# Squares behind both heads' products, probabilities' low parts last, and the merged half turned one tick sooner, in a two-layer hybrid encoder

## The chip, the cores and the metric

The kernel runs on one core of a Trainium2 chip. Its time is the device time of one execution in microseconds (us). The engines are named as in the profile: PE multiplies matrices, PEld is its weight load, DVE is the vector engine, ACT the scalar engine, POOL is GpSimd, and SP issues most transfers.

## The reference

256 tokens of 1024 channels pass through two layers. The part that matters here, for each layer:

```python
u = rms_norm(h, g_mix_pre)
(gq, gk, gv, gg, ra_f, ra_b, aq, ak, av, gate_a, gate_b) = jnp.split(u @ w_in, offsets, axis=-1)
# branch A: gated linear attention (GLA), 4 heads of 256 values, both directions summed
o_gla = rms_norm(o_f + o_b, g_gla_out).reshape(b, s, GLA_VAL)   # a root for each head and token
branch_a = (o_gla * jax.nn.silu(gg)) @ w_o_gla
# branch B: 8 query heads of 128 on 2 key/value heads
pr = jax.nn.softmax(sc, axis=-1)
out = jnp.einsum('bkgqs,bskd->bqkgd', pr, v)
branch_b = out @ w_o_attn
# merge
mixed = jax.nn.sigmoid(gate_a) * branch_a + jax.nn.sigmoid(gate_b) * branch_b
h = h + rms_norm(mixed @ w_out, g_mix_post)
```

A SwiGLU feed-forward part and a per-layer embedding follow; the change does not touch them.

## The kernel before

Tokens lie in two halves (`hf`) of 128. Every matrix product of full accuracy is three products: each operand is split into a high part (rounded to the matrix engine's 32-bit format) and the low rest, and high × high, high × low and low × high are added up in one PSUM tile. `split` (L133) makes the parts: ACT casts the high one, DVE subtracts to get the low one. `mm3` (L105) multiplies one pair of operands so; `passes` (L121) does it for a list of pairs, and puts the products of one operand's low parts behind all the others. A weight arrives by DMA as 128x1024 pieces, is split into wh and wl, and is used in blocks of twelve matmuls of 128x512 (four pieces of the contraction by three products).

The work of a layer stands in the program in the order rq, kv, gqk, v, gg, gate, merge, wout, ffnin, ffnout, ple; the names in the profile end in these (acc_0wout is a PSUM accumulator of layer 0's output projection). Beside this main row run tasks, Python generators that are taken a step further by `tick()`: it is called twice in each block of twelve matmuls, once in the middle and once at the end, and a task that has yielded n goes on n ticks later. So attention (`at`), the GLA outputs (`gla`) and the out-gate are threaded between the projections' blocks. A scheduler of the framework then orders the instructions on each engine, so that a step that the program moves by a line may end elsewhere in an engine's row. Eight PSUM banks serve all accumulators; the framework keeps two engines from using one tile at the same time by waits.

The three places that the change touches:

- **GLA outputs.** `outputs(hf, pr)` takes one PSUM tile (aux_0gla) for the two heads of a pair: six matmuls of 128x256 for each head, each followed by an ACT Square with a sum over the row (L1345). Both sums go to POOL for the root (`inv_sqrt`, L465 and L466), and DVE multiplies each head by its root and a gain (`scale_gain`, L515) into big_0gla. There are four such tiles in a layer. Behind them the out-gate (`out_gate`) waits for all outputs and the attention: ACT loads its table and takes the Sigmoid of gg (L1406), DVE multiplies (L126) gg and big_0gla into it, and PE transposes the result (L447, aux_0gg) for the product with w_o_gla.
- **Attention.** `attend` multiplies the values with the transposed probabilities, whose halves (mid_0at) were split just before: two `mm3` for the two halves of the keys, into aux_0at; four such tiles in a layer.
- **Merge.** `merge(1)` multiplies the second branch by its gate and adds (L1469) into the first; a task `turn` then waits `WAIT_MIX[hf]` ticks and transposes this quarter (L447, aux_0merge), and splits it into big_0merge, the operand of the output projection acc_0wout.

Of the kernel before, what the change touches and what calls it, by code (L numbers as in the profile page):

```python
# [13 lines left out]
AF = mybir.ActivationFunctionType  # L14
# [3 lines left out]
P = 128  # L18
# [8 lines left out]
WAIT, WAIT_FIRST, WAIT_FFN, WAIT_BLOCK = 6, 4, 4, 6  # L27

WAIT_NEXT, WAIT_IN, WAIT_H = (7, 9), ((6, 9), (6, 6)), ((3, 5), (3, 5))
WAIT_MIX = 4, 6  # L30
WAIT_SPREAD = 12
W = dict(r=5, z=6, s0=4, s=3, s1=9, o0=1, o=1, k=4, q=3, a0=1, a1=4, a2=4, a3=1, g=6)

# [26 lines left out]
def trunk_kernel(ctx: ExitStack, tc: tile.TileContext, a: dict, out: bass.AP):  # L60
# [25 lines left out]
    def big(dt=F32):  # L86
        return bigp.tile([P, 2048], dt, tag="big", name=nm("big"))

    def mid(dt=F32):
        return b4p.tile([P, 1024], dt, tag="mid", name=nm("mid"))  # L90

    def acc():
        return accp.tile([P, 512], F32, tag="acc", name=nm("acc"))

    def aux():
        return accp.tile([P, 512], F32, tag="acc", name=nm("aux"))
# [4 lines left out]
    def small(n, tag, bufs=None):  # L101
        return smp.tile([P, n], F32, tag=tag, name=nm(tag), **({"bufs": bufs} if bufs else {}))

    def mm(o, lhsT, rhs, start, stop):
        return nc.tensor.matmul(o, lhsT, rhs, start=start, stop=stop)  # L105

    def mm3(o, l, r, start, stop):
        (lh, ll), (rh, rl) = l, r
        mm(o, lh, rh, start, False)
        mm(o, lh, rl, False, False)  # L110
        mm(o, ll, rh, False, stop)

    def passes(o, parts, start, stop, fresh=False, between=None, **kw):

        ps = [((xh, yh), (xh, yl), (xl, yh)) if fresh else ((xh, yh), (xl, yh), (xh, yl)) for (xh, xl), (yh, yl) in parts]
        seq = [p for t in ps for p in t[:2]] + [t[2] for t in ps]
        for n, (x, y) in enumerate(seq):  # L120
            nc.tensor.matmul(o, x, y, start=start and n == 0, stop=stop and n == len(seq) - 1, **kw)  # L121
            if between is not None and 2 * (n + 1) == len(seq):
                between()
# [7 lines left out]
    def split(hi, lo, src):  # L131

        return nc.scalar.copy(hi, src), nc.vector.tensor_tensor(out=lo, in0=src, in1=hi.bitcast(F32), op=ALU.subtract)  # L133
# [325 lines left out]
    def inv_sqrt(t, n, mul, add, eps=None):  # L459

        with in_turn():
            if eps is None:
                nc.gpsimd.tensor_scalar(out=t, in0=t, scalar1=mul, scalar2=add, op0=ALU.mult, op1=ALU.add)
            else:
                nc.gpsimd.tensor_scalar(out=t, in0=t, scalar1=eps, scalar2=mul, op0=ALU.add, op1=ALU.mult)  # L465
        last_pow[0] = nc.gpsimd.tensor_tensor(out=t, in0=t, in1=neghalf[:, :n], op=ALU.pow)  # L466
# [47 lines left out]
    def scale_gain(out, in0, r, g):  # L514
        nc.vector.scalar_tensor_tensor(out=out, in0=in0, scalar=r, in1=g, op0=ALU.mult, op1=ALU.mult)  # L515

    def halves(t):
        return [t[:, j * 512 : (j + 1) * 512] for j in range(2)]
# [205 lines left out]
    def project_t(sp):  # L724

        o = [acc(), acc()]
        for kh in range(2):
            wmode(o, sp, kh * 4, ws.take(), kh == 0, kh == 1)
            ws.done()
        return o  # L730

    def project(sp):

        o = [acc(), acc()]
        for kh in range(2):
            w = ws.take()
            for hf in range(2):
                amode(o[hf], sp, hf, kh * 4, w, kh == 0, kh == 1)
            ws.done()
        return o  # L740
# [81 lines left out]
    ss = [small(2, "ss") for _ in range(2)]  # L822
# [179 lines left out]
    for l in range(DEPTH):  # L1002
# [104 lines left out]
        o = {}  # L1107
# [18 lines left out]
        kTh, kTl, avh, avl = (kv4[:, i * 512 : (i + 1) * 512] for i in range(4))  # L1126
# [39 lines left out]
        def softmax(g, hf, q):  # L1166
            qh, ql, sc = q
            pr_ = mid().rearrange("p (h k) -> p h k", k=T)
            for b in range(2):
                s_ps = aux()  # L1170
                for i in range(2):
                    hs = slice((2 * b + i) * P, (2 * b + i + 1) * P)
                    gs = slice(g * T, (g + 1) * T)
                    mm3(s_ps[:, i * T : (i + 1) * T], (qh[:, hs], ql[:, hs]), (kTh[:, gs], kTl[:, gs]), True, True)
                mx = small(2, "mx")
                nc.vector.tensor_reduce(
                    out=mx, in_=s_ps.rearrange("p (h k) -> p h k", k=T), axis=AX.X, op=ALU.max
                )
                nc.vector.scalar_tensor_tensor(
                    out=mx, in0=mx, scalar=-1.0, in1=sc[:, 2 * b : 2 * b + 2], op0=ALU.mult, op1=ALU.mult  # L1180
                )
                sm = small(2, "sm")
                for i in range(2):
                    hd = 2 * b + i
                    last_exp[0] = nc.scalar.activation(
                        pr_[:, hd, :], s_ps[:, i * T : (i + 1) * T], AF.Exp,
                        bias=mx[:, i : i + 1], scale=sc[:, hd : hd + 1], accum_out=sm[:, i : i + 1],
                    )
                nc.vector.reciprocal(sm, sm)
                for i in range(2):  # L1190
                    hd = 2 * b + i
                    nc.vector.tensor_scalar(
                        out=pr_[:, hd, :], in0=pr_[:, hd, :], scalar1=sm[:, i : i + 1], scalar2=None, op0=ALU.mult
                    )
            return pr_

        def turn_p(pr_):
            res = []
            for s in range(2):
                ps = aux()  # L1200
                for i in range(4):
                    nc.tensor.transpose(ps[:, i * P : (i + 1) * P], pr_[:, i, s * P : (s + 1) * P], ident)
                pT = halves(mid(F32R))
                split(pT[0], pT[1], ps)
                res.append(pT)
            return res

        def attend(g):
            qs = []
            for hf in range(2):  # L1210
                yield W["q"]
                ps = aux()
                for i in range(4):
                    hd = 4 * g + i
                    nc.tensor.transpose(ps[:, i * P : (i + 1) * P], qrs[hf][:, hd * P : (hd + 1) * P], ident)
                qh, ql = halves(mid(F32R))
                split(qh, ql, ps)
                qs.append((qh, ql, qss[hf][:, 4 * g : 4 * g + 4]))
            keys.need()
            yield W["a0"]  # L1220
            prs = []
            for hf in range(2):
                prs.append(softmax(g, hf, qs[hf]))
                yield W["a1"]
            for hf in range(2):
                pT = turn_p(prs[hf])
                yield W["a2"]
                o = aux()
                for s in range(2):
                    vs = slice(s * 256 + g * P, s * 256 + (g + 1) * P)  # L1230
                    mm3(o, (avh[:, vs], avl[:, vs]), pT[s], s == 0, s == 1)
                aT.put(o, 4 * g, 4, hf * P, P)
                yield W["a3"]

        def attention():
            for g_ in range(2):
                part[0] = f"{l}at{g_}"
                yield from attend(g_)
# [9 lines left out]
        for x in range(2):  # L1248
            o = project_t(uT)
# [81 lines left out]
        on = big().rearrange("p (s c) -> p s c", s=2)  # L1331

        def outputs(hf, pr):

            o = aux()
            ss = small(8, "hss")
            for i in range(2):
                hd = 2 * pr + i
                c = slice(hd * 256, (hd + 1) * 256)
                oh = o[:, i * 256 : (i + 1) * 256]  # L1340
                for s in range(2):

                    idx = hf if s == hf else (2 if s == 0 else 3)
                    mm3(oh, [t[:, hd, idx, :] for t in sc], [t[:, s, c] for t in v], s == 0, s == 1)
                nc.scalar.activation(  # L1345
                    on[:, hf, c], oh, AF.Square, scale=1.0 / 16.0, accum_out=ss[:, i : i + 1]
                )
            inv_sqrt(ss[:, 0:2], 2, 1.0, EPS, eps_out[hf])
            for i in range(2):
                hd = 2 * pr + i  # L1350
                scale_gain(
                    on[:, hf, hd * 256 : (hd + 1) * 256], o[:, i * 256 : (i + 1) * 256], ss[:, i : i + 1], ggla
                )
# [39 lines left out]
        for j in range(2):  # L1393
            o = project(uT)
# [69 lines left out]
        def merge(br):  # L1464
            def then(j, hf, o):
                sl = [s[:, hf, j * 512 : (j + 1) * 512] for s in sgate[: br + 1]]
                vmul(sl[br], o, sl[br])
                if br == 1:
                    nc.vector.tensor_tensor(out=sl[0], in0=sl[0], in1=sl[1], op=ALU.add)  # L1469

                    def turn():
                        yield WAIT_MIX[hf]
                        transpose_in(mixT, sl[0], 4 * j, 4, hf)
# [57 lines left out]
        for hf in range(2):  # L1531
            ws.lend = hf == 1
            for b in range(2):
                o = acc()
# [51 lines left out]
        o = []  # L1586
# [140 lines left out]
```

## Time and profile before

| | us |
|---|---|
| three runs | 922.91, 920.76, 922.87 |
| their median | 922.87 |
| the profiled execution: own time | 921.4 |
| its span | 919.3 |
| PE busy in the span | 910.1 |
| DVE busy | 786.2 |
| ACT busy | 584.7 |
| POOL busy | 105.1 |

The span goes from the first to the last instruction of the profiled execution; 2.1 us of that execution's own time lie around it. The granted clock of the matrix engine was 0.997 of full speed. In the rows of the timeline the columns are start, duration, engine, line, operation, written tile and read tiles, shapes and the number of instructions in the group; the bracket at the end is the engine's idle time ahead of the group, with what ended it. Matmuls overlap in their pipeline, so a group of n takes n − 1 distances between starts and one duration.

### The profile page before, as it was taken

Reading aid. Unit: us, or ns where it says so; the run is one execution under the profiler, and the core shown is the slowest. Engines: PE = TensorE matmul, PEld = TensorE weight load, DVE = VectorE, ACT = ScalarE, POOL = GpSimd, SP = SyncE. Lnnn points to the kernel's source line nnn. Section 1 sums busy time; section 2 is a strip of 40 time slices with the busy share of each in tenths; the row PEclk is TensorE's granted clock in tenths of the full one; section 3 lists DMA queues with packets and bytes.
Section 4 is the critical chain, followed back from the end, with each engine's and each line's share of the span. In section 5 each row is a group of like instructions: output and inputs, shape, how many; then the busy total and the mean of one; then the engine's idle time right before and its main releaser. Section 6 shows DMA issues by size and latency. Waiting matters only on the chain.

```text
span 919.3 us, 12437 instructions
## 1 busy us (share of the span) xinstructions
PE 910.1 (99%) x4674; PEld 775.9 (84%) x4674; DVE 786.2 (86%) x1007; ACT 584.7 (64%) x970; POOL 105.1 (11%) x156
## 2 busy tenths in 40 slices
PE   9999999999999999999999999999999999999996
PEld 8998888888888888888899988888888788888886
DVE  6898979987669998999779789799876899989885
ACT  6688767564467565566676687675644766565563
POOL 3610212310000000000334002210001000000000
PEclk9999999999999999999999999999999999999998
DMA  8564445657385655657567424455573846556361
GB/s 280 192 209 136 138 138 189 212 184 250 104 293 183 215 194 185 246 167 254 175 255 230 138 92 140 135 183 183 186 255 121 279 165 215 213 174 223 135 232 46
DMA packets 88679, 173.44 MB, mean 189 GB/s; under 512 B 3422, under 2 KB 26470, under 8 KB 88108
## 3 DMA queue, kind: packets, MB, share of 16 engines
q1 hardware_dynamic: 88316, 172.27, 55.5%
q8 instruction: 36, 0.59, 0.3%
q10 hardware_dynamic: 304, 0.40, 0.1%
q14 instruction: 23, 0.19, 0.1%
HBM read 169.50 MB, written 3.15 MB: 188 GB/s over the span
## 4 chain that ended last, share of the span: by engine, by line
PE 93%; DVE 2%; ACT 1%; issue 1%; DMA 1%; POOL 1%; POOLq 0%; ACTq 0%; DVEq 0%; SPq 0%
PE acc_0ffnin L121 12%; PE acc_1ffnin L121 11%; PE acc_1gate L121 7%; PE acc_0gate L121 7%; PE acc_0ffnin L105 7%; PE acc_1ffnin L105 7%; PE acc_1rq L121 3%; PE acc_0gqk L121 2%; PE acc_0wout L121 2%; PE acc_1gqk L121 2%; PE acc_0ple L121 2%; PE acc_0v L121 2%; PE acc_1merge L121 2%; PE acc_0merge L121 2%; PE acc_1ple L121 2%; PE acc_0gg L121 2%
## 5 line engine op out<-in xcount | busy, mean ns | idle before, releaser
L105 PE MATMUL acc_0ffnin<-wh_0ffnin,big_0ffnin 128*128 128x512 f32 x176 | 57.0, 393 | 0.0
L105 PE MATMUL acc_1ffnin<-wh_1ffnin,big_1ffnin 128*128 128x512 f32 x176 | 56.9, 392 | 0.0
L133 ACT CAST wh_1ffnin<-raw_1ffnin 128x1024 fp32r<-128x1024 f32 x38 | 38.5, 1049 | 25.7 <-PE acc_1ffnin L105 10.3
L133 ACT CAST wh_0ffnin<-raw_0ffnin 128x1024 fp32r<-128x1024 f32 x38 | 38.2, 1048 | 24.5 <-PE acc_0ffnin L105 9.2
L133 DVE TENSOR_TENSOR wl_1ffnin<-raw_1ffnin,wh_1ffnin 128x1024 fp32r<-128x1024 f32 x38 | 44.9, 1219 | 7.9 <-ACT wh_1ffnin L133 7.6
L133 DVE TENSOR_TENSOR wl_0ffnin<-raw_0ffnin,wh_0ffnin 128x1024 fp32r<-128x1024 f32 x38 | 44.7, 1220 | 8.0 <-ACT wh_0ffnin L133 8.0
L121 PE MATMUL acc_1ffnin<-wh_1ffnin,big_1wout 128*128 128x512 f32 x168 | 42.5, 393 | 0.0
L121 PE MATMUL acc_0ffnin<-wh_0ffnin,big_0wout 128*128 128x512 f32 x168 | 42.5, 393 | 0.0
L105 PEld LDWEIGHTS acc_0ffnin<-wh_0ffnin,big_0ffnin 128*128 128x128 f32 x176 | 33.0, 188 | 7.2 <-DVE big_0ffnin L133 0.4
L105 PEld LDWEIGHTS acc_1ffnin<-wh_1ffnin,big_1ffnin 128*128 128x128 f32 x176 | 33.0, 188 | 6.8
L133 DVE TENSOR_TENSOR wl_1ffnin<-lent_1ffnin,wh_1ffnin 128x1024 fp32r<-128x1024 f32 x30 | 35.7, 1215 | 1.8 <-ACT wh_1ffnin L133 1.7
L133 DVE TENSOR_TENSOR wl_0ffnin<-lent_0ffnin,wh_0ffnin 128x1024 fp32r<-128x1024 f32 x30 | 35.7, 1216 | 1.7 <-ACT wh_0ffnin L133 1.7
L121 PEld LDWEIGHTS acc_1ffnin<-wh_1ffnin,big_1wout 128*128 128x128 f32 x168 | 31.1, 188 | 6.2
L121 PEld LDWEIGHTS acc_0ffnin<-wh_0ffnin,big_0wout 128*128 128x128 f32 x168 | 31.1, 188 | 6.2
L133 ACT CAST wh_1ffnin<-lent_1ffnin 128x1024 fp32r<-128x1024 f32 x30 | 30.7, 1052 | 7.5 <-PE acc_1ffnin L105 3.9
L133 ACT CAST wh_0ffnin<-lent_0ffnin 128x1024 fp32r<-128x1024 f32 x30 | 30.7, 1053 | 6.6 <-PE acc_0ffnin L105 3.9
L105 PE MATMUL acc_0ffnin<-wl_0ffnin,big_0ffnin 128*128 128x512 f32 x88 | 34.3, 389 | 0.0
L105 PE MATMUL acc_1ffnin<-wl_1ffnin,big_1ffnin 128*128 128x512 f32 x88 | 34.3, 389 | 0.0
L133 DVE TENSOR_TENSOR wl_1gate<-raw_1gate,wh_1gate 128x1024 fp32r<-128x1024 f32 x20 | 23.5, 1219 | 6.5 <-ACT wh_1gate L133 6.4
L133 DVE TENSOR_TENSOR wl_0gate<-raw_0gate,wh_0gate 128x1024 fp32r<-128x1024 f32 x20 | 24.2, 1256 | 5.3 <-ACT wh_0gate L133 5.2
L133 ACT CAST wh_1gate<-raw_1gate 128x1024 fp32r<-128x1024 f32 x20 | 20.0, 1049 | 13.2 <-DMA raw_1gate<-in_w_o_attn_dram 6.2
L133 ACT CAST wh_0gate<-raw_0gate 128x1024 fp32r<-128x1024 f32 x20 | 20.1, 1050 | 12.9 <-DMA raw_0gate<-in_w_o_attn_dram 6.3
(720 smaller groups left out, 2719.9 us busy)
## 6 DMA issues: line engine op xcount, KB each, us to landing
raw_0ffnin<-in_w_ffn_out_dram SPq DMA_DIRECT2D x11, 1024.0 KB, 5.7
raw_1ffnin<-in_w_ffn_out_dram SPq DMA_DIRECT2D x11, 1024.0 KB, 5.2
lent_0ffnin<-in_w_ffn_in_dram SPq DMA_DIRECT2D x6, 1024.0 KB, 7.6
lent_1ffnin<-in_w_ffn_in_dram SPq DMA_DIRECT2D x6, 1024.0 KB, 6.6
raw_0v<-in_w_in_dram SPq DMA_DIRECT2D x4, 1024.0 KB, 5.0
raw_0gate<-in_w_o_gla_dram SPq DMA_DIRECT2D x4, 1024.0 KB, 5.1
raw_0gate<-in_w_o_attn_dram SPq DMA_DIRECT2D x4, 1024.0 KB, 5.5
raw_0wout<-in_w_ffn_in_dram SPq DMA_DIRECT2D x8, 512.0 KB, 5.5
```

Source lines behind the costliest of these rows:

```text
L105: return nc.tensor.matmul(o, lhsT, rhs, start=start, stop=stop)
L121: nc.tensor.matmul(o, x, y, start=start and n == 0, stop=stop and n == len(seq) - 1, **kw)
L133: return nc.scalar.copy(hi, src), nc.vector.tensor_tensor(out=lo, in0=src, in1=hi.bitcast(F32), op=ALU.subtract)
```

## The change

It has three parts, and both layers run them. The two heads' Squares of a GLA tile are issued behind both heads' products instead of each behind its own. The probabilities' product in `attend` goes through `passes` instead of two `mm3`, which puts the two products with the probabilities' low parts last. And the merged quarters of the first half of the tokens are transposed three ticks after they are made instead of four.

```diff
-WAIT_MIX = 4, 6
+WAIT_MIX = 3, 6
...
                 o = aux()
-                for s in range(2):
-                    vs = slice(s * 256 + g * P, s * 256 + (g + 1) * P)
-                    mm3(o, (avh[:, vs], avl[:, vs]), pT[s], s == 0, s == 1)
+                vs = [slice(s * 256 + g * P, s * 256 + (g + 1) * P) for s in range(2)]
+                passes(o, [((avh[:, c], avl[:, c]), pT[s]) for s, c in enumerate(vs)], True, True)
                 aT.put(o, 4 * g, 4, hf * P, P)
...
                     mm3(oh, [t[:, hd, idx, :] for t in sc], [t[:, s, c] for t in v], s == 0, s == 1)
+            for i in range(2):
+                c = slice((2 * pr + i) * 256, (2 * pr + i + 1) * 256)
                 nc.scalar.activation(
-                    on[:, hf, c], oh, AF.Square, scale=1.0 / 16.0, accum_out=ss[:, i : i + 1]
+                    on[:, hf, c], o[:, i * 256 : (i + 1) * 256], AF.Square, scale=1.0 / 16.0, accum_out=ss[:, i : i + 1]
                 )
             inv_sqrt(ss[:, 0:2], 2, 1.0, EPS, eps_out[hf])
```

The first place is the PE's row at the first and second GLA tile of layer 0 (numbers tell tiles of one name apart; acc_0gg is the projection whose blocks the outputs stand between):

```order
-L121 MATMUL acc_0gg_1447<-wh_0gg_1372,big_start_279 128x512 x2
-L121 MATMUL acc_0gg_1447<-wl_0gg_1373,big_start_279 128x512
 L105 MATMUL aux_0gla_1528<-v_0v_1008,big_0gla_1171 128x256
 L105 MATMUL aux_0gla_1528<-v_0v_1009,big_0gla_1171 128x256
...
 L105 MATMUL aux_0gla_1528<-v_0v_1009,big_0gla_1171 128x256
 L105 MATMUL aux_0gla_1528<-v_0v_1008,big_0gla_1172 128x256
-L121 MATMUL acc_0gg_1447<-wl_0gg_1373,big_start_279 128x512 x3
+L121 MATMUL acc_0gg_1447<-wh_0gg_1372,big_start_279 128x512 x2
+L121 MATMUL acc_0gg_1447<-wl_0gg_1373,big_start_279 128x512 x4
 L105 MATMUL aux_0gla_1554<-v_0v_1008,big_0gla_1171 128x256
```

The three matmuls of acc_0gg that stood between the two heads of tile 1528 now stand behind both, undivided, ahead of tile 1554; the same happens at the other tiles and in layer 1.

The second place is ACT's row over the last two GLA tiles (1580 and 1606) of layer 0, before:

```order
137 L133 COPY mid_0gate_1659<-mid_0gate_1652 128x512
138 L1345 ACTIVATE big_0gla_965,hss_0gla_1581<-aux_0gla_1580 128x256
139 L133 COPY wh_0gg_1626<-raw_0gg_1443 128x1024 x2
140 L1345 ACTIVATE big_0gla_965,hss_0gla_1581<-aux_0gla_1580 128x256
141 L1397 ACTIVATE big_0gg_1312<-acc_0gg_1448,rs_start_121 128x512
142 L1345 ACTIVATE big_0gla_965,hss_0gla_1607<-aux_0gla_1606 128x256
143 L1406 ACT_TABLE_LOAD
144 L1406 ACTIVATE mid_0gg_1672<-big_0gg_1312 128x1024
145 L1345 ACTIVATE big_0gla_965,hss_0gla_1607<-aux_0gla_1606 128x256
146 L133 COPY big_0at_1497<-aux_0at_1642 128x4x128
147 L1406 ACTIVATE mid_0gg_1678<-big_0gg_1312 128x1024
```

and after:

```order
137 L133 COPY mid_0gate_1659<-mid_0gate_1652 128x512
138 L1407 ACT_TABLE_LOAD
139 L1407 ACTIVATE mid_0gg_1672<-big_0gg_1312 128x1024
140 L1346 ACTIVATE big_0gla_965,hss_0gla_1581<-aux_0gla_1580 128x256 x2
141 L133 COPY wh_0gg_1626<-raw_0gg_1443 128x1024
142 L1346 ACTIVATE big_0gla_965,hss_0gla_1607<-aux_0gla_1606 128x256 x2
143 L133 COPY wh_0gg_1626<-raw_0gg_1443 128x1024
144 L1398 ACTIVATE big_0gg_1312<-acc_0gg_1448,rs_start_121 128x512
145 L133 COPY big_0at_1497<-aux_0at_1642 128x4x128
146 L1407 ACTIVATE mid_0gg_1678<-big_0gg_1312 128x1024
```

The squares stand in pairs, the table load and the first Sigmoid (L1406 before, L1407 after) have moved ahead of the squares of both tiles, and the cast of wh_0gg is divided by the last pair. On DVE, one half of the low part wl_0gg_1627 moves from ahead of the fourth tile's L515 to behind it, and some subtractions (L129) move ahead of the third tile's L515.

The third place is PE's row at the output projection of layer 0, where the second quarter of the first half (aux_0merge_2371 before, aux_0merge_2358 after) is transposed; acc_0wout_2338 and 2339 belong to the first half of the tokens. Before:

```order
379 L121 MATMUL acc_0wout_2339<-wh_0merge_2218,big_0merge_2257 128x512 x6
380 L975 MATMUL aux_0emb_2358<-ident,mid_0wout_2335 128x128 x4
381 L121 MATMUL acc_0wout_2339<-wh_0merge_2218,big_0merge_2257 128x512 x2
382 L121 MATMUL acc_0wout_2339<-wl_0merge_2219,big_0merge_2257 128x512 x4
383 L447 MATMUL aux_0merge_2371<-ident,big_0gate_1780 128x128 x4
384 L447 MATMUL aux_0merge_2391<-ident,big_0gate_1780 128x128 x4
385 L121 MATMUL acc_0wout_2432<-wh_0merge_2182,big_0merge_2257 128x512
386 L121 MATMUL acc_0wout_2338<-wh_0merge_2260,big_0merge_2376 128x512
```

and after:

```order
384 L121 MATMUL acc_0wout_2339<-wh_0merge_2218,big_0merge_2251 128x512 x6
385 L447 MATMUL aux_0merge_2358<-ident,big_0gate_1780 128x128 x4
386 L975 MATMUL aux_0emb_2366<-ident,mid_0wout_2335 128x128 x4
387 L121 MATMUL acc_0wout_2339<-wh_0merge_2218,big_0merge_2251 128x512 x2
388 L121 MATMUL acc_0wout_2339<-wl_0merge_2219,big_0merge_2251 128x512 x4
389 L121 MATMUL acc_0wout_2338<-wh_0merge_2260,big_0merge_2363 128x512
```

The transposes of that quarter move six matmuls ahead, and those of the other half (2391) leave this place for one behind the next blocks of acc_0wout_2338. In `attend`, six matmuls of a tile went high 0, values' low 0 and probabilities' low 0, and then the same for half 1; now the two products with the probabilities' low parts are the fifth and the sixth. The rows of POOL and SP hold the same instructions in the same order as before.

## The prediction

> **What bounds the kernel now.** I read the page's first and fourth parts, then the wait lists of the matrix engine, then the timeline at the three places the change touches, and last the busy time of the stage behind the first of them. The page:
>
> ```profile
> span 919.3 us, 12437 instructions
> PE 910.1 (99%) x4674; PEld 775.9 (84%) x4674; DVE 786.2 (86%) x1007; ACT 584.7 (64%) x970; POOL 105.1 (11%) x156
> PE 93%; DVE 2%; ACT 1%; issue 1%; DMA 1%; POOL 1%; POOLq 0%; ACTq 0%; DVEq 0%; SPq 0%
> ```
>
> PE is busy for 910.1 of 919.3 us and makes up 93 % of the chain that ended last. No matmul is added or removed, so the change can only win back time that PE loses at the touched places, or lose some elsewhere. The idle time of the weight loads shows where it waits (line, producer, us in total, times, longest):
>
> ```profile
> PEld aux_0gla L105 <- ACT big_0gla L1345: 1.5, 4, 0.6
> PEld aux_1gla L105 <- ACT big_1gla L1345: 1.5, 4, 0.6
> PEld aux_1at L105 <- DVE mid_1at L133: 0.6, 1, 0.6
> PEld acc_1wout L121 <- ACT big_1merge L133: 0.3, 1, 0.3
> PEld acc_0wout L121 <- ACT big_0merge L133: 0.3, 1, 0.3
> ```
>
> All five rows belong to the three edits. Together they are 4.2 us of weight-load idleness; but a weight load normally overlaps the matmul before it, so what PE itself loses has to be read from starts and groups.
>
> **Part 1, the squares.** Before, head 1's six products in a tile wait for the Square of head 0, which reads the same tile. The first, second, third and fourth such waits in layer 0:
>
> ```profile
> 128.89 0.39 PE L121 MATMUL acc_0gg<-wl_0gg,big_start 128*128 128x512 f32 x1
> 129.15 0.78 PEld L105 LDWEIGHTS aux_0gla<-v_0v,big_0gla 128*128 128x128 f32 x6 [0.30 <-ACT big_0gla L1345]
> 129.15 0.98 PE L105 MATMUL aux_0gla<-v_0v,big_0gla 128*128 128x256 f32 x6
> 130.67 0.87 PE L105 MATMUL aux_0gla<-v_0v,big_0gla 128*128 128x256 f32 x6
> 131.38 0.86 PE L121 MATMUL acc_0gg<-wh_0gg,big_start 128*128 128x512 f32 x3
> 132.10 0.98 PE L105 MATMUL aux_0gla<-v_0v,big_0gla 128*128 128x256 f32 x6
> 134.80 0.62 PE L121 MATMUL acc_0gg<-wl_0gg,big_start 128*128 128x512 f32 x2
> 135.58 0.62 PE L105 MATMUL aux_0gla<-v_0v,big_0gla 128*128 128x256 f32 x3 [0.16 <-ACT big_0gla L1345]
> 137.58 1.33 PE L121 MATMUL acc_0gate<-wh_0gg,big_start 128*128 128x512 f32 x5
> 138.78 0.98 PE L105 MATMUL aux_0gla<-v_0v,big_0gla 128*128 128x256 f32 x6
> ```
>
> A 128x512 matmul alone shows 0.39 us and two in a row 0.62, so one starts every 0.23 us (0.227 from the group of five: (1.33 − 0.39) / 4 gives 0.235, of three (0.86 − 0.39) / 2 gives 0.235; the pitch is 0.23). An undisturbed six of 128x256 takes 0.87, a waiting one 0.98: 0.11 lost inside each group. The start of the group is late by 129.15 − 128.89 − 0.23 = 0.03, by 132.10 − 131.38 − 0.69 = 0.03, by 135.58 − 134.80 − 0.46 = 0.32 and by 138.78 − 137.58 − 1.15 = 0.05 us. The sum is 0.43 + 4 × 0.11 = 0.87 us a layer, far less than the 1.5 of the wait list. Layer 1 has the same row in that list, so I take 0.87 there too: 1.74 us. After the change the twelve products run without that wait. The blocks of 128x512 matmuls that stood between the heads stay, undivided, between the tiles.
>
> What hides the rest of the loss is the queue ahead of the array. The Trainium skill, "TensorE: Matmul & The Clock Gate", section "Architectural detail: the array is 16× 32×32, not 1× 128×128", says that the engine can pull weight loads ahead of matmuls in flight. By that rule only the late starts, 0.43 us a layer, would be lost and the sum would be 0.9 us smaller; the waiting groups of 0.98 against 0.87 us do not bear it out for the matmuls right behind a wait.
>
> What it costs lies behind. The root on POOL needs both squares of a tile, and the multiplication on DVE (L515) needs the root. ACT now runs the table load and the first Sigmoid ahead of the third and the fourth tile's squares, and DVE takes half of a weight's low part (wl_0gg) behind the fourth L515, where it stood before it. Rows for this, in the order of time; the last is a stretch with PE, PEld, DVE, ACT and POOL busy:
>
> ```profile
> 134.54 0.62 ACT L133 CAST mid_0gate<-mid_0gate 128x512 fp32r<-128x512 f32 x1 [0.94 <-DVE mid_0gate L126]
> 135.43 1.98 ACT L133 CAST wh_0gg<-raw_0gg 128x1024 fp32r<-128x1024 f32 x2
> 138.75 1.28 ACT L1406 ACT_TABLE_LOAD   x1
> 140.04 1.06 ACT L1406 ACTIVATE mid_0gg<-big_0gg 128x1024 f32<-128x1024 f32 x1
> 141.01 0.36 ACT L1345 ACTIVATE big_0gla<-aux_0gla 128x256 f32<-128x256 f32 x1
> 141.10 1.21 DVE L133 TENSOR_TENSOR wl_0gg<-raw_0gg,wh_0gg 128x1024 fp32r<-128x1024 f32 x1
> 141.56 1.40 POOL L465 TENSOR_SCALAR hss_0gla<-hss_0gla,em_start 128x2 f32<-128x2 f32 x1 [1.29 <-ACT big_0gla L1345]
> 144.10 0.88 DVE L515 SCALAR_TENSOR_TENSOR big_0gla<-aux_0gla,hss_0gla,ggla_0gla 128x256 f32<-128x256 f32 x2 [0.59 <-POOL hss_0gla L466]
> 149.71 0.68 DVE L126 TENSOR_TENSOR mid_0gg<-mid_0gg,big_0gla 128x512 f32<-128x512 f32 x1
> 150.51 1.90 PEld L447 LDWEIGHTS aux_0gg<-ident,mid_0gg 128*128 128x128 f32 x16
> 159.58 2.35 DVE L133 TENSOR_TENSOR wl_0gate<-raw_0gate,wh_0gate 128x1024 fp32r<-128x1024 f32 x2
> 162.26 0.87 PEld L121 LDWEIGHTS acc_0gate<-wl_0gate,big_start 128*128 128x128 f32 x4
> 141.40:163.00 21.60, 21.60 (x105) 18.09 (x105) 21.01 (x29) 15.33 (x22) 2.42 (x2) 1.00 0.54 198
> ```
>
> In the new order ACT has the cast (to 134.54 + 0.62 = 135.16), the load and the Sigmoid (to 137.50), the third tile's two squares (0.55 each with the reading of the sum, as from 141.01 to POOL's start at 141.56; to 138.60), half of a weight's cast (0.99; to 139.59) and the fourth tile's squares, done at 140.69 instead of 141.56: 0.87 sooner, as much as PE. The fourth L515 follows, at 144.10 − 0.87 = 143.23. Behind it DVE has the 6.29 us up to 150.39, and now 1.21 more: 150.73 for the last product of the out-gate. Only the last four of sixteen transposes read it; sixteen take 1.90 us, so these begin at 150.51 − 0.87 + 12 × 0.11 = 150.96 and wait for nothing. But DVE is now 0.34 us behind its old times where PE is 0.87 ahead, and it has no room: it is busy for 21.01 of 21.60 us, 0.59 to spare. The next place is the low part of the gate's third weight: ready 161.93, 0.33 ahead of the four matmuls (162.26) that read it. Its second half, for the third and fourth of them, would be ready at about 162.2, less the 0.0 to 0.59 that DVE's idle time gives back, and is wanted at 162.26 − 0.87 + 2 × 0.23 = 161.85. So PE loses 0 to 0.4 by this working; the other end, with ACT's chain 0.9 later than worked (its 0.94 us wait for DVE may grow as well as go), is 1.3 a layer. I take 0.4 a layer, the end of the worked rows: 0.8 in all.
>
> **Part 2, low parts last.** It stalls once in eight places, in layer 1:
>
> ```profile
> 543.37 1.28 DVE L133 TENSOR_TENSOR mid_1at<-aux_1at,mid_1at 128x512 fp32r<-128x512 f32 x2
> 543.52 0.39 PE L105 MATMUL aux_1at<-mid_1at,big_1kv 128*128 128x512 f32 x1
> 544.10 1.43 PE L105 MATMUL aux_1at<-mid_1at,big_1kv 128*128 128x512 f32 x5 [0.19 <-DVE mid_1at L133]
> 139.83 1.54 PE L105 MATMUL aux_0at<-mid_0at,big_0kv 128*128 128x512 f32 x6
> ```
>
> Undisturbed, six take 1.54 us; here they take 544.10 + 1.43 − 543.52 = 2.01, so 0.47 is lost. The two low parts are done about half way and at the end of DVE's 1.28 us, at 544.01 and 544.65. In the new order the first is wanted by the fifth matmul (543.52 + 4 × 0.23 = 544.44) and the second by the sixth (544.67, its weights some 0.2 sooner). The first wait goes; the second can cost 0 to 0.25. I take a gain of 0.35. The seven other places lose nothing now and only want the low parts later.
>
> **Part 3, the merged half one tick sooner.** A tick is six matmuls, 1.38 us.
>
> ```profile
> 228.05 0.69 DVE L1469 TENSOR_TENSOR big_0gate<-big_0gate,big_0gate 128x512 f32<-128x512 f32 x1
> 232.83 1.03 PE L447 MATMUL aux_0merge<-ident,big_0gate 128*128 128x128 f32 x8
> 233.46 1.08 ACT L133 CAST big_0merge<-aux_0merge 128x512 fp32r<-128x512 f32 x2 [1.19 <-PE aux_0merge L447]
> 233.62 0.98 PE L121 MATMUL acc_0wout<-wh_0merge,big_0merge 128*128 128x512 f32 x2
> 691.81 0.98 PE L121 MATMUL acc_1wout<-wh_1merge,big_1merge 128*128 128x512 f32 x2
> ```
>
> The pair of matmuls behind the transposes takes 0.98 instead of 0.62 us in both layers: the second wants a half that ACT is still casting. That is 0.36 a layer. Moved six matmuls ahead (to about 229.9, with the merged half ready at 228.05 + 0.69 = 228.74), the transposes have 1.38 us of matmuls to hide the cast, which ends (233.46 + 0.54 − 232.83) = 1.17 us after the transposes begin. ACT waits 1.19 us for them today, so it is free. The stall goes: 0.72 in all. SP's and POOL's orders are the same as before.
>
> **The sum.** 1.74 − 0.8 + 0.35 + 0.72 = 2.0 us gained: 921.4 (the profiled execution's own time) becomes 919.4. The runs were 922.91, 920.76 and 922.87, so the profiled one lies 1.5 under their median; against the median, 922.87 − 2.0 gives 920.9. A measurement of this kernel can tell about 0.3 %, 2.8 us, from no change, so the forecast lies within it. At best nothing is given back and part 2 wins all: 1.74 + 0.47 + 0.72 = 2.9 us.
>
> **Rivals.**
> *All the stalls go* (chance 0.25). For it: DVE's 0.59 us of idle time in the gate stage, and the 0.94 us that ACT waited ahead of its cast, in which the load can start sooner. Against it: DVE's 21.01 of 21.60 us. 922.87 − 2.9 = 920.0, just over 0.3 % faster.
> *The gate stage keeps PE to DVE's pace* (0.22). DVE ends where it ended, so of part 1 only the old slack of 0.33 us a layer stays: 0.66 + 0.35 + 0.72 = 1.7, less up to 0.7 for DVE's 0.34 in each layer: 1.0. That gives 921.9.
> *The squares come too late* (0.13). The third tile's squares stand behind 1.28 + 1.06 us on ACT that they did not stand behind before. If the load starts only when it did (138.75) instead of at 135.16, the roots come 138.75 − 135.16 = 3.59 us later than worked, the low part of the gate's weight with them, and PE waits 0.4 + 3.59 = 4.0 us a layer. It decides the sign once the wait is over 0.87 + (0.35 + 0.72) / 2 = 1.4 us a layer. At its whole price it costs 2 × (4.0 − 1.4) = 5.2 us: 928.1. Against it: what the load stood behind at 138.75, the squares and the weight's cast, is put behind it now.
> *The change does not shorten PE* (0.05): each stall comes back at the next wait for the same producer; 922.9.
>
> **How the numbers follow.** The forecast itself has 0.35. Faster by over 0.3 %: most of the first rival (0.22) and the forecast's edge (0.08), 0.30. Slower by over 0.3 %: the late squares from half their price up, 0.09. The rest, 0.61, is within. The range goes from the fastest of the three runs with every stall gone (920.76 − 2.9 = 917.9) to 0.8 us over the median (923.7), which takes in the second and the fourth rival, and the late squares up to a wait of 1.8 us a layer; above it lies 0.1 and below it, for what no row shows, 0.05.
>
> **What would show it.** After: no wait of aux_0gla or aux_1gla on the squares in the weight loads' list, and groups of twelve in about 1.6 us; the pairs at wout in 0.62; the six of aux_1at under 1.8. The transposes at L447 in the gate stage begin 0.9 us sooner without a gap ahead of them, and a wait of up to 0.4 us appears at the low part of the gate's third weight. I am wrong if PE waits at either place for more than 0.9 us, if the table load is not the first thing behind the cast, or if PE's busy time and its gaps together shrink by more than 2.9 us.

## The result, and the profile after

The changed kernel takes 918.48 us (median of six runs, 918.09 to 919.59); the kernel before, in six runs, 921.91. The ratio is 0.9963, with a 95 % interval from 0.9951 to 0.9976: 3.4 us faster, between 2.2 and 4.5. That lies in the stated range (917.9 to 923.7), but the forecast's own gain, 2.0 us, lies below that interval, and the ratio is just over the 0.3 % within which the forecast had put it (the interval reaches to both sides of 0.3 %). What came is nearest to the first rival, "all the stalls go", from which the lower end of the range had been made.

The page of the kernel after has the same work in a shorter span:

```profile
span 916.4 us, 12439 instructions
PE 908.1 (99%) x4674; PEld 776.5 (85%) x4674; DVE 786.2 (86%) x1007; ACT 584.1 (64%) x970; POOL 102.4 (11%) x156
PE 96%; DVE 2%; issue 1%; ACT 0%; POOLq 0%; POOL 0%; DVEq 0%; ACTq 0%
```

In the list of what the weight loads wait for, the five rows of before have shrunk to one, aux_1at (0.6 has become 0.3). Its rows around it (dots: rows left out):

```profile
PEld acc_0ffnin L105 <- DVE big_0ffnin L133: 0.5, 1, 0.5
...
PEld aux_1wout L447 <- DVE mid_1wout L515: 0.3, 1, 0.3
PEld aux_1at L121 <- DVE mid_1at L133: 0.3, 1, 0.3
PEld aux_1wout L447 <- PE aux_1wout L447: 0.3, 1, 0.3
```

The timeline after, at the places whose rows of before the prediction shows:

```profile
130.19 1.59 PE L105 MATMUL aux_0gla<-v_0v,big_0gla 128*128 128x256 f32 x12
133.01 1.59 PE L105 MATMUL aux_0gla<-v_0v,big_0gla 128*128 128x256 f32 x12
230.58 0.70 PE L121 MATMUL acc_0wout<-wh_0merge,big_0merge 128*128 128x512 f32 x2
542.31 1.68 PE L121 MATMUL aux_1at<-mid_1at,big_1kv 128*128 128x512 f32 x6
```

Twelve products run undivided in 1.59 us, the pair at wout takes 0.70 instead of 0.98, the six of the attention tile 1.68 instead of 2.01. The gate stage, where the forecast saw 0.8 us given back:

```profile
141.82 0.87 DVE L515 SCALAR_TENSOR_TENSOR big_0gla<-aux_0gla,hss_0gla,ggla_0gla 128x256 f32<-128x256 f32 x2
147.95 1.28 DVE L126 TENSOR_TENSOR mid_0gg<-mid_0gg,big_0gla 128x512 f32<-128x512 f32 x2
149.30 1.90 PEld L447 LDWEIGHTS aux_0gg<-ident,mid_0gg 128*128 128x128 f32 x16
158.43 2.35 DVE L133 TENSOR_TENSOR wl_0gate<-raw_0gate,wh_0gate 128x1024 fp32r<-128x1024 f32 x2
161.06 0.87 PEld L121 LDWEIGHTS acc_0gate<-wl_0gate,big_start 128*128 128x128 f32 x4
```

No bracket: nothing waits. The gate's low part is ready at 160.78 (158.43 + 2.35), 0.28 us ahead of the first of the weight loads; before it was 0.33 ahead. DVE came forward by 1.15 us, nearly as far as PE (1.20).

For all the experiments one reading is made from the records of the 4,674 matmuls: for each, the distance to the next start less the undisturbed distance for its shape (0.227 us for 128x512, 0.120 for 128x256, about 0.11 for transposes), summed by place. It is the time that PE lost there, in us, in one profiled execution each (a value just below nothing means that a few distances were shorter than the undisturbed one):

| kernel | start | GLA 0 | gate 0 | wout 0 | attention 1 | GLA 1 | gate 1 | wout 1 | ahead of ffnin 1 | all |
|---|---|---|---|---|---|---|---|---|---|---|
| before | 0.95 | 0.93 | -0.08 | 0.41 | 0.48 | 0.92 | -0.06 | 0.38 | 0.73 | 6.3 |
| after | 0.60 | 0.07 | -0.08 | 0.16 | 0.17 | 0.08 | -0.08 | 0.19 | 0.50 | 3.6 |
| only_squares | 0.63 | 0.07 | -0.08 | 0.41 | 0.49 | 0.08 | -0.08 | 0.37 | 0.73 | 5.5 |
| only_lows | 0.66 | 0.92 | -0.08 | 0.41 | 0.16 | 0.93 | -0.07 | 0.37 | 0.74 | 5.7 |
| only_merge | 0.62 | 0.93 | -0.08 | 0.16 | 0.48 | 0.92 | -0.07 | 0.14 | 0.50 | 5.3 |
| load_late | 0.81 | 0.07 | -0.08 | 0.16 | 0.18 | 0.08 | -0.08 | 0.14 | 0.52 | 3.5 |
| gain_x2 | 0.74 | 0.07 | -0.03 | 0.16 | 0.17 | 0.08 | -0.06 | 0.14 | 0.52 | 3.5 |
| gain_x3 | 1.04 | 0.07 | 0.74 | 0.17 | 0.17 | 0.08 | 0.73 | 0.14 | 0.51 | 5.9 |
| in_7 | 0.74 | 0.07 | -0.08 | 0.17 | 0.16 | 0.08 | -0.08 | 0.13 | 0.06 | 2.9 |
| mix_2 | 0.56 | 0.07 | -0.07 | 0.16 | 0.16 | 0.08 | -0.07 | 0.13 | 0.50 | 3.8 |
| two_tiles | 0.66 | 0.07 | 0.76 | 0.41 | 0.50 | 0.08 | 0.78 | 0.37 | 0.73 | 6.4 |

The places not shown hold the rest, 1.6 to 2.9 us. The start (first transfers and casts) and the feed-forward parts vary by some tenths, once by 1.2 us, between executions without any pattern in the edits.

### The profile page after: what moved, and what is told of

It is laid out like the page before. It is cut to its first block, busy times and chain, and to the rows that moved or that the text cites. A ratio compares the mean times of both kernels' runs of the same rounds, so it can differ in the third digit from the quotient of the medians.

```text
span 916.4 us, 12439 instructions
## 1 busy us (share of the span) xinstructions
PE 908.1 (99%) x4674; PEld 776.5 (85%) x4674; DVE 786.2 (86%) x1007; ACT 584.1 (64%) x970; POOL 102.4 (11%) x156
## 4 chain that ended last, share of the span: by engine, by line
PE 96%; DVE 2%; issue 1%; ACT 0%; POOLq 0%; POOL 0%; DVEq 0%; ACTq 0%
PE acc_1ffnin L121 12%; PE acc_0ffnin L121 11%; PE acc_1gate L121 7%; PE acc_0gate L121 7%; PE acc_1ffnin L105 7%; PE acc_0ffnin L105 6%; PE acc_1rq L121 3%; PE acc_0gqk L121 3%; PE acc_1gqk L121 3%; PE acc_1wout L121 2%; PE acc_0wout L121 2%; PE acc_0ple L121 2%; PE acc_1gg L121 2%; PE acc_0gg L121 2%; PE acc_1v L121 2%; PE acc_0v L121 2%
```

## The experiments

**Each part alone.** The three kernels are the kernel before with one hunk of the change each.

> The first part of the change alone. Theory A (the waits on the Squares go and the gate stage gives nothing back): PE's distances between starts lose nothing beside the GLA tiles, both layers together gain 1.6 to 1.7 us against the kernel before, and no wait for DVE appears at the transposes of the gate stage or at the low part of the gate's weight. Theory B (the step of the prediction: the gate stage gives 0.4 us a layer back): 0.8 to 0.9 us gained, with a wait of about 0.4 us a layer at the low part of the gate's weight.

Measured: 919.52 us against 921.08 of the kernel before, which was run again beside each experiment, ratio 0.9981 (0.9971 to 0.9991). PE's loss at the GLA tiles falls by 0.86 and 0.84 us, and the gate stages lose nothing: theory A. In this profiled execution one wait of 1.0 us in the last feed-forward part, which no other kernel has at that length, hides half of the gain; by place the part is worth 1.7 us.

> The second part alone. Theory A: the six matmuls of the first attention tile of layer 1 take 1.68 us instead of 2.01, the 0.3 us are the whole gain, and the seven other tiles change by nothing. Rival: the later low products delay the attention's output and the gain is lost behind, 0 us.

Measured: 920.55 against 921.08, ratio 0.9996 (0.9987 to 1.0005), by the interval not told from no change. By place 0.32 us, and nothing else moves: theory A as far as the trace goes.

> The third part alone. Theory A: the pair of matmuls behind the transposes at wout takes 0.6 to 0.7 us instead of 0.98 in both layers, 0.6 us gained in all. Rival: the transposes ahead of time cost as much in changed neighbours as the wait did, 0 us.

Measured: 920.67 against 921.08, ratio 0.9995 (0.9987 to 1.0004), again not told from no change. By place 0.25 and 0.24 us at wout, and 0.23 more ahead of layer 1's feed-forward part, where the kernel before lost 0.73; the other two parts alone leave that 0.73 as it is. So the third part has a second, unforeseen place, and is worth 0.7 in all.

The three sum to 1.70 + 0.32 + 0.72 = 2.7 us by place, and after shows 2.7 less than before in the last column. (The start's 0.35 and a loss of 0.25 in the first feed-forward part nearly cancel.)

**Is the load's new place needed?** In the changed kernel, the Sigmoid is ordered behind the last Square, which last_sq holds:

```diff
-                nc.scalar.activation(
+                last_sq[0] = nc.scalar.activation(
...
-                with tc.issue_after(last_exp[0].ins):
+                with tc.issue_after(last_sq[0].ins):
                     nc.scalar.activation(sg, gg[:, hf, :], AF.Sigmoid)
```

> The changed kernel, with the out-gate's table load and first Sigmoid ordered behind the last Square on ACT, as they nearly stood before; PE's row is the same, and DVE takes both halves of the low part wl_gg ahead of the fourth L515. Theory A (what brings DVE forward is the earlier end of the tiles on PE; the load's place is not needed): within 0.3 us of the changed kernel, about 918.5. Theory B (the load ahead of the squares is what keeps DVE ahead of PE): DVE falls back to its pace of before, the low part of the gate's weight comes 0.5 to 0.6 us late in each layer, 919.6.

Measured: 918.09 against 921.08, ratio 0.9972 (0.9962 to 0.9982); PE loses nothing in the gate stages. By the time it is theory A: neither the load ahead of the squares nor half of wl_gg behind the fourth L515 is needed to keep DVE in time. Theory A's own reason, that the earlier end of the tiles on PE brings DVE forward, is not shown by that; two_tiles below speaks against it.

**How much room has DVE left?** In the changed kernel, the two L515 of the last tile are done two or three times:

```diff
-                scale_gain(
-                    on[:, hf, hd * 256 : (hd + 1) * 256], o[:, i * 256 : (i + 1) * 256], ss[:, i : i + 1], ggla
-                )
+                for _ in range(2 if hf == 1 and pr == 1 else 1):
+                    scale_gain(
+                        on[:, hf, hd * 256 : (hd + 1) * 256], o[:, i * 256 : (i + 1) * 256], ss[:, i : i + 1], ggla
+                    )
```

> The changed kernel, with the two L515 of the last GLA tile done twice, 0.83 us more of DVE in each layer's gate stage; PE's, ACT's and POOL's rows are the same. Theory A (DVE has no time left there and the low part of the gate's weight is 0.3 us ahead of PE): PE waits 0.5 us a layer, 1.0 us slower than the changed kernel. Theory B (DVE has room that the stretch doesn't show): 0 us.

Measured: 918.05 against 920.95, ratio 0.9968 (0.9956 to 0.9979): as fast as the changed kernel. A stretch in which DVE is busy throughout is no proof that it has no room. The same window of after and, in the second row, of this run (its length, then busy time and instructions of PE, PEld, DVE, ACT and POOL, then the clock and the DMA):

```profile
140.20:161.80 21.60, 21.60 (x105) 18.09 (x104) 21.60 (x29) 16.18 (x23) 0.69 (x1) 1.00 0.49 182
140.20:161.80 21.60, 21.60 (x106) 18.07 (x104) 21.60 (x31) 16.43 (x23) 0.89 (x2) 1.00 0.49 181
```

DVE is busy for 21.60 of 21.60 us in both, and 0.83 us more work was done with nothing lost in time: DVE works ahead of PE, and what counts is the lead of each product over its reader. Here the lead is nearly used up: a weight load of layer 1 begins to wait for the gate's low part.

```profile
PEld acc_1gate L121 <- DVE wl_1gate L133: 0.2, 1, 0.2
```

Theory A fell by its size: I had taken the lead over the first of the four matmuls, 0.3 us, for the room of the stage. The low part comes in two halves, and the second one is read by the third and the fourth matmul. In after it is ready at 160.78, and the third weight load starts two distances behind 161.06, at 161.51: the lead that counts is 0.73 us. The scheduler also moved one of DVE's subtractions behind other work.

> The changed kernel, with the two L515 of the last GLA tile done three times, 1.66 us more of DVE in each layer. Theory A: PE waits 1.66 - 0.3 = 1.4 us a layer, 2.7 us slower than the changed kernel. Theory B: below 1 us.

Measured: 919.89 against 920.95, ratio 0.9989 (0.998 to 0.9998), 1.8 us over gain_x2, less than the 2.7 of theory A and more than theory B. PE loses 0.8 us more in each gate stage, 1.6 us in all, and most of it at the transposes, where the working of the prediction had found no wait:

```profile
149.97 1.47 PE L447 MATMUL aux_0gg<-ident,mid_0gg 128*128 128x128 f32 x12
151.16 0.68 DVE L126 TENSOR_TENSOR mid_0gg<-mid_0gg,big_0gla 128x512 f32<-128x512 f32 x1
151.90 0.66 PE L447 MATMUL aux_0gg<-ident,mid_0gg 128*128 128x128 f32 x4 [0.46 <-DVE mid_0gg L126]
```

Twelve of the sixteen transposes run, the last four wait for the out-gate's last product. So the room in the gate stage of the changed kernel is about 0.8 us a layer: 0.83 is all but free, and of 1.66 about 0.8 is paid.

**The same wait removed in another way.** The kernel before, with the heads of a pair in two tiles; the Squares stay where they were:

```diff
-            o = aux()
+            o = [aux()[:, 0:256] for _ in range(2)]
...
-                oh = o[:, i * 256 : (i + 1) * 256]
+                oh = o[i]
```

> The kernel before, with the two heads of a GLA output in two PSUM tiles instead of one; the Squares stay where they were in the program. Theory A (PE waited only because the Square reads the tile that the second head's products write): the waits on the Squares go as in the changed kernel, PE loses under 0.1 us beside the GLA tiles of each layer, 1.6 us gained against the kernel before. Rival: four more of the eight banks' tiles are wanted in the same stretch, and PE waits for a bank instead, 0 us or slower.

Measured: 921.36 against 921.14, ratio 1.0005 (0.9996 to 1.0014). PE's row at the GLA tiles is that of the changed kernel, twelve products undivided, and its loss there is 0.07 and 0.08 us. All of the gain is given back in the gate stages, 0.84 us each. No bank was short; the wait is for DVE:

```profile
PEld acc_1gate L121 <- DVE wl_1gate L133: 1.0, 2, 0.8
PEld acc_0gate L121 <- DVE wl_0gate L133: 1.0, 2, 0.8
...
160.09 2.35 DVE L133 TENSOR_TENSOR wl_0gate<-raw_0gate,wh_0gate 128x1024 fp32r<-128x1024 f32 x2
162.49 0.72 PE L121 MATMUL acc_0gate<-wl_0gate,big_start 128*128 128x512 f32 x2 [0.40 <-DVE wl_0gate L133]
```

Theory A was right on the wait and wrong on the time, and the rival was wrong on the resource. This is the mechanism of the prediction's second rival, that the gate stage keeps PE to DVE's pace, and it takes more than that rival had said: not even the old slack of 0.33 us a layer stays, because the low part starts 32.74 us behind the first GLA product, 0.8 us later than before (31.95). What differs from the changed kernel is DVE's row. The busy times in the 22 us from the first GLA product (first three rows: before, after and two_tiles), and in the 9 us behind them (last three, in the same order):

```profile
127.63:149.63 22.00, 21.84 (x119) 18.09 (x117) 18.31 (x31) 13.96 (x30) 7.25 (x8) 1.00 0.57 191
127.28:149.28 22.00, 22.00 (x122) 19.17 (x121) 19.04 (x33) 16.16 (x34) 5.56 (x8) 1.00 0.66 228
127.35:149.35 22.00, 22.00 (x122) 19.16 (x121) 17.54 (x30) 15.01 (x31) 6.21 (x8) 1.00 0.65 223
149.63:158.63 9.00, 9.00 (x49) 7.68 (x48) 9.00 (x12) 8.60 (x14) 0.00 (x0) 1.00 0.36 133
149.28:158.28 9.00, 9.00 (x49) 7.69 (x48) 9.00 (x11) 6.67 (x10) 0.00 (x0) 1.00 0.12 42
149.35:158.35 9.00, 9.00 (x49) 7.56 (x48) 9.00 (x13) 8.02 (x12) 0.00 (x0) 1.00 0.14 54
```

In the first 22 us DVE idles for 3.69 us before, 2.96 after and 4.46 in two_tiles, nearly all of it waiting for the roots (in two_tiles 0.69 for a cast of ACT); in the 9 us behind them it is busy throughout in all three. It waits for four roots before and in two_tiles and for three after; what it has in hand meanwhile differs. In two_tiles four subtractions of the gate's sums (L129, 0.6 us from start to start) stand behind the fourth L515, in the changed kernel all four are done ahead of the third, and only half of a weight's low part (1.21 us) stands behind the fourth:

```profile
142.87 0.68 DVE L129 TENSOR_TENSOR mid_0gate<-mid_0gate 128x512 f32<-128x512 f32 x1
143.58 0.69 DVE L129 TENSOR_TENSOR t_0gate<-mid_0gate,mid_0gate 128x512 f32<-128x512 f32 x1
145.40 0.68 DVE L129 TENSOR_TENSOR mid_0gate<-mid_0gate,t_0gate 128x512 f32<-128x512 f32 x1
149.61 0.68 DVE L129 TENSOR_TENSOR mid_0gate<-mid_0gate,mid_0gate 128x512 f32<-128x512 f32 x1
```

Those rows are of two_tiles. The order of these steps alone is not decisive: in load_late two of the four subtractions stand behind the fourth L515, and nothing is lost. The idle time is, together with the lead of 0.73 us. The rows where the gate's low part starts in gain_x2 and, behind the dots, in gain_x3:

```profile
127.55 1.68 PE L105 MATMUL aux_0gla<-v_0v,big_0gla 128*128 128x256 f32 x12
159.48 2.35 DVE L133 TENSOR_TENSOR wl_0gate<-raw_0gate,wh_0gate 128x1024 fp32r<-128x1024 f32 x2
...
127.72 1.68 PE L105 MATMUL aux_0gla<-v_0v,big_0gla 128*128 128x256 f32 x12
160.44 2.35 DVE L133 TENSOR_TENSOR wl_0gate<-raw_0gate,wh_0gate 128x1024 fp32r<-128x1024 f32 x2
```

All times in the table are of layer 0, in us; the third column counts from the first GLA product, and the last two are against after:

| kernel | DVE idle in the 22 us | low part starts | later by | PE loses more in the gate stage |
|---|---|---|---|---|
| after | 2.96 | 31.15 | 0 | 0 |
| only_squares | 2.95 | 31.14 | 0 | 0 |
| load_late | 3.24 | 31.43 | 0.28 | 0 |
| gain_x2 | 2.97 | 31.93 | 0.78 | 0.05 |
| gain_x3 | 2.96 | 32.72 | 1.57 | 0.82 |
| two_tiles | 4.46 | 32.74 | 1.59 | 0.84 |

Where DVE does no extra work, its low part is later by about as much as it idled more: in load_late 0.28 us of both, in two_tiles 1.50 of idling and 1.59. Parts 2 and 3, which only_squares and two_tiles both lack, have no share in it. And whatever made it late, PE pays what goes beyond 0.73 to 0.75 us, which is the lead of the second half over its reader. Why the scheduler leaves DVE more idle in two_tiles is read from the rows above; no run puts after's order on DVE into two_tiles.

**Two small steps on.** Both start from the changed kernel: layer 1's second half turned one tick later ahead of its feed-forward part, and the merged quarters one tick sooner still.

```diff
-WAIT_NEXT, WAIT_IN, WAIT_H = (7, 9), ((6, 9), (6, 6)), ((3, 5), (3, 5))
+WAIT_NEXT, WAIT_IN, WAIT_H = (7, 9), ((6, 9), (6, 7)), ((3, 5), (3, 5))
```

> The changed kernel, with the second half's transposes ahead of the feed-forward part of layer 1 one tick (six matmuls) later (WAIT_IN 6 to 7 there). After the change PE loses 0.32 us at them to L515 on DVE and 0.3 us between the two groups. If both go and nothing waits behind: 0.3 to 0.5 us faster than the changed kernel. Rival: what the transposes feed is then late, 0 us or slower.

Measured: 918.27 against 920.95, ratio 0.9971 (0.996 to 0.9981). By place 0.44 us go (0.50 to 0.06) and nothing waits behind. The trace has the least loss of all, 2.9 us, but by time it is not told from the changed kernel.

```diff
-WAIT_MIX = 3, 6
+WAIT_MIX = 2, 6
```

> The changed kernel, with the merged quarters of the first half of the tokens turned yet one tick sooner (WAIT_MIX 3 to 2). Theory A (the wait at wout was for ACT's cast, and one tick covers it whole): no wait was left, so 0 us. Rival: the transposes now come ahead of the merged quarter, and PE waits for L1470 by some tenths of a us.

Measured: 917.93 against 920.95, ratio 0.9969 (0.9957 to 0.9981), and no place of the table differs from the changed kernel by more than 0.06: theory A. One tick covers the cast whole, a second adds nothing.

## Why the prediction was right or wrong

The time fell into the range, but not by the forecast's own sum: one term of it was wrong, and the range was wide enough for the rival without that term.

**The gross gain of part 1 was right**: 1.74 us worked, 1.70 measured by place. The late starts and the slow groups both went. That speaks against the rule of the Trainium skill ("TensorE: Matmul & The Clock Gate", "Architectural detail: the array is 16× 32×32, not 1× 128×128") as the prediction had used it: by weight loads pulled ahead only 0.43 us a layer would have been lost and won, and 0.85 was.

**The term that failed is the 0.4 us a layer given back in the gate stage; it was nothing.** Its mechanism exists (two_tiles shows it in full, gain_x3 at another place), but its size here was wrong, in two steps of the working. All times of after below are moved by 0.35 us, since its GLA stage began that much sooner. The fourth tile's squares were to be done at 140.69 and were done at 139.73 + 0.35 = 140.08: neighbours on ACT overlap (the third tile's second square starts at 137.59, before the reading of the first one's sum ends at 137.69), so that a pair of squares with the readings of its sums takes 0.82 us, not 1.10. And the fourth L515 was put 2.54 us behind the squares, as before, but POOL's two steps took 0.97 us and not 2.42, so that the root was ready at 141.25, ahead of DVE. L515 did not wait for it; it began when DVE was done with the first half of wl_gg, at 142.17 instead of 143.23. The last out-gate product ended at 149.58 instead of 150.73, and the gate's low part began at 158.78: 0.8 us sooner than before, where the working had it 0.3 later. Its second half was ready 0.73 us ahead of its reader, where the working had it 0.4 behind. The fixed points of the working (the order on ACT, the place of half of wl_gg) were as said; the durations that I carried over from before depend on what runs beside them.

**A second fault is in the reasoning.** "21.01 of 21.60 us busy" was read as a lack of room. In the changed kernel a stretch of the same length is busy for 21.60 of 21.60, and 0.83 us more still fitted. The idle time that mattered lay ahead of that stretch, in the waits for the roots, and there the change recovers 0.73 us of DVE (3.69 against 2.96), most of it because the fourth L515 no longer waits for its root (0.59 before).

**Part 2 was right, part 3 in size by luck.** Part 2: 0.35 worked, 0.31 measured, with the second low part costing 0.16 as bounded. Part 3: 0.72 worked, 0.7 measured, but two errors cancel. A pair behind transposes takes 0.70 undisturbed, not 0.62, as a row of the kernel before could have told, so only 0.25 a layer was won there:

```profile
231.35 0.71 PE L121 MATMUL acc_0wout<-wh_0merge,big_0merge 128*128 128x512 f32 x2
```

The other 0.23 came at the transposes ahead of layer 1's feed-forward part, which the prediction did not look at; by which route an earlier merged quarter reaches them is not followed up here.

**The squares did not come too late**: the load ran at 134.97, right behind the cast, as worked, and not at 138.75. Where the load stands did not matter either, as load_late shows.

That the medians differ by 3.4 us where the places give 2.7 is within the interval; what the start and the feed-forward parts add in one execution or another is not settled.

## What to carry to other kernels

A wait removed from the bounding engine is worth what it cost only if the engine behind it comes forward by as much. Look there for the idle time of the second engine in the stretch *ahead* of where it is full, and for the lead of each of its products over the instruction that reads it, piece by piece, rather than for its busy share: two kernels with the same row on PE at the GLA tiles differed by 0.84 us a layer through what DVE had in hand while it waited. And durations of small steps that wait on a neighbour should not be carried from one order to another.

## What the runs showed of the hardware

POOL's first step for a root (L465, two columns wide) lasts from 0.27 to 1.89 us, and a long one ends when a DVE instruction beside it ends. From after and, behind the line of dots, from load_late:

```profile
138.15 0.93 POOL L465 TENSOR_SCALAR hss_0gla<-hss_0gla,em_start 128x2 f32<-128x2 f32 x1 [3.29 <-ACT big_0gla L1346]
138.34 0.69 DVE L129 TENSOR_TENSOR mid_0gate<-mid_0gate,t_0gate 128x512 f32<-128x512 f32 x1
139.85 0.27 POOL L465 TENSOR_SCALAR hss_0gla<-hss_0gla,em_start 128x2 f32<-128x2 f32 x1
139.89 0.88 DVE L515 SCALAR_TENSOR_TENSOR big_0gla<-aux_0gla,hss_0gla,ggla_0gla 128x256 f32<-128x256 f32 x2 [0.86 <-POOL hss_0gla L466]
...
138.70 2.35 DVE L133 TENSOR_TENSOR wl_0gg<-raw_0gg,wh_0gg 128x1024 fp32r<-128x1024 f32 x2
139.21 1.89 POOL L465 TENSOR_SCALAR hss_0gla<-hss_0gla,em_start 128x2 f32<-128x2 f32 x1 [1.34 <-ACT big_0gla L1348]
```

The first ends at 139.08 with L129 (139.03), the last at 141.10 with the low part (141.05). Beside L515, which has one of its two large operands in PSUM, the step takes 0.27, as it does where DVE idles. The Trainium skill, "SBUF — State Buffer", section "Who interferes with whom", states it: an instruction of VectorE with two inputs in SBUF contends with one of GpSimd that reads SBUF, and one with at most one such input, outside the 2-port modes, does not. The traces agree: of the 54 longer rows of L465 in the eleven kernels, 50 end 0.05 or 0.06 us behind an instruction of DVE beside them and four about 0.13 behind. By that rule the root in the changed kernel is short because the half of wl_gg and the subtraction that had run beside the fourth tile's root (141.56, 1.40 us) no longer do. The short root is not needed for the gain: load_late has the longest one, and PE loses nothing there.
